# Cached sequences' attention: pages taken unsplit into float32 products, four sequences in four strips of 32 array columns

## The chip, the core and the metric

One NeuronCore of a Trainium2 chip runs one program. TensorE (PE; PEld is its weight load) multiplies, VectorE (DVE), ScalarE (ACT) and GpSimd (POOL) do the element work, and SyncE (SP) issues the transfers. The metric is the device time of one execution in microseconds (us), lower is better.

## The reference, cut to what matters

One step of a two-layer decoder for a prompt of 1024 tokens and for 8 sampled sequences of 4 new tokens. The first layer's mixer has a differential attention: four heads, two maps of 64 channels each, values of 128 channels. Each of the 8 sequences also attends to 2048 cached tokens, in 16 pages of 128 that a page table names:

```python
s = jnp.einsum('bqhcd,bkhcd->bhcqk', q.astype(jnp.float32), k.astype(jnp.float32)) * scale
s = jnp.where(visible, s, -jnp.inf)
p = jax.nn.softmax(s, axis=-1)
w = p[:, :, 0] - lam * p[:, :, 1]
return jnp.einsum('bhqk,bkhe->bqhe', w, v.astype(jnp.float32))
```

A page holds 128 tokens by 512 numbers (four heads by two maps by 64, or four heads by 128), 256 KB. All 128 pages of keys and 128 pages of values are read once, in float32. Beside the attention the mixer has a convolution branch; then come an output product, an MLP, the second layer (a state-space mixer) and its MLP.

## The kernel before, in words

Nearly all products are made of float32r parts: a number is split into a high part of 12 bits (a copy to float32r on ScalarE) and the rest (a subtraction on VectorE or GpSimd), and each product becomes two or three products of parts. Tiles of [128, 1056] ("slabs", 48 of them) hold everything; eight banks of PSUM hold [128, 512] each.

The first layer's attention has three streams, which `mixer0` starts at lines 1495 to 1513. The main line is `prompt` (the prompt's own attention, block by block: scores `sp`, maximum and exponential, weights `p`, their transposes `wT`, outputs `av`). Beside it run generators that `pump` advances by rates: `decode_k` (rate RK), `decode_v` (rate RV), the softmax `dec_softmax` between them, and later `conv_half`, the convolution's part of the output product. The generators set the order in which work is written; a scheduler with a model of the engines then sets each engine's final order.

`decode_k`, in steps of two pages of one sequence: the pages `pg` are turned (`kT`, eight transposes, L920), the high parts copied from PSUM (`pgh`, L923), the low parts subtracted (`pgl`, L929). The 32 rows of queries of one sequence (8 per head: two maps by four tokens) stand with high and low parts, and with the places of two sequences, in 128 columns of weights (`QB`); per head one product with the high keys (L963) and one with the low (L964), 256 keys wide, add up in the bank `sc`. Two sequences share 64 rows. ScalarE copies the half of the high queries (L968), VectorE adds that of the low ones (L969). After 32 of the 64 steps four sequences' scores stand in `SA` and `SB`, and `dec_softmax` makes their weights, transposes them and splits them (`PT`, L1087, L1088), 64 columns per sequence.

`decode_v`, in steps of two pages of one sequence: high copy (L995, ScalarE), low subtraction (L999, by turns on GpSimd and VectorE), then per page two products of 64 columns of weights with 512 values (L1034, L1035), all adding up in the bank `O` of that sequence. `heads_of` picks the heads' blocks out.

Of the kernel before, what the change touches and what calls it, by code (L numbers as in the profile page):

```python
# [16 lines left out]
P = 128  # L17
# [31 lines left out]
class Step:  # L49
# [34 lines left out]
    def V(self, n):  # L84
        """n columns of a slab that is kept while any of it is in use"""
        if self.vn + n > T:
            self.vs, self.vn = self.S("keep"), 0
        v = self.vs[:, self.vn:self.vn + n]
        self.vn += n
        return v  # L90

    def dma(self, out, in_):
        """a transfer of the queue that keeps the order of the program"""
        i = self.nc.sync.dma_start(out, in_)
        self.tc.keep_in_program_order(i)
        self.last_dma = i.ins
        return i

# [34 lines left out]
    def gains(self, names):  # L133
        """generator: the gains' loads, then the gains on the feature axis"""
# [18 lines left out]
    def newton(self, out, m):  # L153
        """out = m ** -0.5: the table's value, and one Newton step; m is used up"""
# [6 lines left out]
    def factor_of(self, out, ssq):  # L161
        """out = -(ssq / D + 1e-6) ** -0.5: the table's value, and one Newton step"""
# [7 lines left out]
    def colsum(self, s, n):  # L170
        """sum over the partitions of s[:, :n], on every partition (in PSUM)"""
# [7 lines left out]
    def wprep(self, src, k, m, eng=None):  # L179
        """weights [128, k, m], split exactly into two float32r parts"""  # L180
# [31 lines left out]
    def split(self, hi, lo, x, scale=None):  # L212
        """hi + lo = x * scale, both of 12 bits"""
# [8 lines left out]
    def x_load(self, c):  # L222
        """the rows of a chunk of x"""
# [9 lines left out]
    def x_factor(self, xs, c, r):  # L233
        """generator: the norm's factor of a chunk's tokens, on every partition; the rows are used up"""
# [19 lines left out]
    def x_rows(self, xs, c, x, r):  # L254
        """generator: a chunk of x on the feature axis: the residual, the split operand, with the factor r or without"""
# [37 lines left out]
    def res_load(self, res, c):  # L293
        """the residual of a chunk: three tiles to a slab"""
# [8 lines left out]
    def post(self, y, c, s, gk, l, h, nxt):  # L303
        """generator: h += rmsnorm(y); for the next layer: its split operand, its factor and the residual"""
# [28 lines left out]
    def end(self, y, c, s, gk, l, h):  # L333
        """generator, a step to each product: the last chunk of the outputs, normed on the token axis"""
# [82 lines left out]
    def factor(self, n):  # L417
        """the norm's factors of the next n chunks"""
# [5 lines left out]
    def chunk_ready(self, c):  # L424
        """before the first products of a stage with a chunk"""
# [11 lines left out]
    def store(self, y, c):  # L437
        """generator: a chunk of the outputs"""
# [16 lines left out]
    def ffn_seq(self, G):  # L455
        """the units of weights in their order: ("u", tile), ("d", first tile, tiles, part). The last sum is of four"""
# [24 lines left out]
    def ffn(self, l, X, r, res, nxt, G, early=None):  # L481
        """squared-ReLU MLP; G: tiles of hidden rows that one sum in PSUM takes"""
# [75 lines left out]
    def gemm_prep(self, w):  # L558
        """the weights of a square product, tile by tile: the first ones ahead of it"""
# [10 lines left out]
    def gemm_post(self, w, Z, gk, l, res, nxt, early=None):  # L570
        """h += rmsnorm(Z w), then what the next layer takes of it"""
# [29 lines left out]
LEADK, LEADV, VM, VP, RK, RV, SMW = 6, 4, 2, (0,), 3.5, 1.5, 6.0  # L601
# [4 lines left out]
VL = ()  # L606
TH, RC, RE = 24, 1.0, 1.0
HL, KA, VA, SL = 17, 2, 2, 1.0
# [3 lines left out]
class Step0(Step):  # L612
    """the attention and convolution mixer of the first layer"""

# [1 line left out]
    def consts0(self):  # L616
        """generator: the loads, then the rest"""
# [19 lines left out]
        # bits of the row: t = p & 3, c = (p >> 2) & 1, s = p >> 5  # L637
# [6 lines left out]
        # first and last column that a row sees: 4 s, 4 s + t  # L644
# [12 lines left out]
        # causal mask of a diagonal block, as a product with the identity  # L657
# [8 lines left out]
        # lambda, on every partition  # L666
# [6 lines left out]
        # gains of the normed heads, of the convolution's norm, both negated, and its taps  # L673
# [16 lines left out]
    def lam(self):  # L690
        """the maps' factors"""
# [3 lines left out]
        # co = -lambda; rowco = 1 or -lambda, by the row's map  # L695
# [7 lines left out]
    def conv_state(self):  # L703
        """generator: the last 30 rows of each sequence, on the channel axis, ahead of the new ones"""
# [17 lines left out]
    def conv(self, k, u, acc):  # L722
        """generator: the 31 taps of one tile of channels"""
# [3 lines left out]
        # the samples: every window against the taps, then the sum  # L727
# [15 lines left out]
    def conv_rest(self, tiles, rest):  # L743
        """generator: the other taps of each tile"""
# [13 lines left out]
    def convs(self, tiles, cd):  # L758
        """generator: the tiles of channels in turn, as they come, then their norm"""
# [20 lines left out]
    def conv_out(self, u):  # L780
        """generator: the convolution's new states"""
# [17 lines left out]
    def rows_rsqrt(self, sq, n, m, r):  # L799
        """generator: r = -(column sums of sq / m + 1e-5) ** -0.5, on every partition; sq is used up"""  # L800
# [13 lines left out]
    def conv_norm(self, acc, s, cd):  # L814
        """generator: layer norm over the channels, silu; s: the channels' sum over the tiles"""
# [25 lines left out]
    def out_units(self, half):  # L841
        """the output product's weights for half of its rows, in units of two tiles of columns"""
# [9 lines left out]
    def conv_half(self, cd, y):  # L852
        """generator: the convolution's part of the output product"""
# [23 lines left out]
    def page_numbers(self, i, n):  # L877
        """entries i to i+n of the page table, for the addresses of transfers"""
# [7 lines left out]
    def pages(self, x, high, low, item):  # L886
# [3 lines left out]
        raw, half, cut = {}, {}, {}  # L890
# [7 lines left out]
        def first(i):  # L898
            if i < 64:
                rw = raw.pop(i)  # L900
                cut[i] = self.S("pgh", F32R), self.S("pgl", F32R)
                half[i] = high(rw, *cut[i])

        def second(i):
            if i < 64:
                low(i, half.pop(i))

        return load, first, second, cut

    def decode_k(self, qs, ks):  # L910
        """generator: the new tokens over the pages of keys. qs: split queries in blocks, ks: the new keys"""
        nc = self.nc

        def high(rw, hi, lo):
            hv, lv = (z[:, :1024].rearrange("p (h j t) -> p h j t", h=4, j=2) for z in (hi, lo))
            parts = []
            for j in range(2):
                pt = self.PS("kT")
                for h in range(4):
                    nc.tensor.transpose(pt[:, h * P:(h + 1) * P], rw[:, 512 * j + h * P:512 * j + (h + 1) * P],  # L920
                                        self.ident)
                pv = pt.rearrange("p (h t) -> p h t", h=4)
                nc.scalar.copy(hv[:, :, j, :], pv)  # L923
                parts.append((lv[:, :, j, :], pv, hv[:, :, j, :]))
            return parts

        def low(i, parts):
            for p in parts:
                nc.vector.tensor_sub(*p)  # L929

        def place(i):
            """the pair of sequences, the step, the sequence of the pair"""
            return i // 16, i % 16 // 2, i % 2

        def item(i):
            sp, pr, e = place(i)
            return 8 * (2 * sp + e) + pr

        load, first, second, cut = self.pages("k", high, low, item)
# [3 lines left out]
        for i in range(KA):  # L943
            first(i)
            second(i)
        for i in range(64):
            g, n = i // 32, i % 32
            load(i + LEADK)
            first(i + KA)
            yield 0.9  # L950
            second(i + KA)
            hi, lo = cut.pop(i)
            sp, pr, e = place(i)
            rows = slice(64 * (sp % 2), 64 * (sp % 2) + 64)
            if n == 0:
                SA, SB = self.S("SA"), self.S("SB")
            q = pr % 2
            if q == 0 and e == 0:
                sc = self.PS("sc")
            for h in range(4):  # L960
                lh = qs[h][:, 2 * sp + e, :]
                o = sc[:, 256 * q:256 * q + 256]
                nc.tensor.matmul(o, lh, hi[:, 256 * h:256 * h + 256], start=e == 0 and h == 0, stop=False)  # L963
                nc.tensor.matmul(o, lh, lo[:, 256 * h:256 * h + 256], start=False, stop=e == 1 and h == 3)  # L964
            if q == 1 and e == 1:
# [1249 lines left out]
```

## Time and profile before

| | us |
|---|---|
| median of 3 runs | 2844.65 (2844.02 to 2846.12) |
| span of the profiled execution, first to last instruction | 2835.7 |
| the stretch of the cached attention in it, from 340 to 712 | 372 |

| engine | busy us | share of the span |
|---|---|---|
| PE | 2607.7 | 92% |
| PEld | 2506.6 | 88% |
| DVE | 1762.2 | 62% |
| ACT | 1101.3 | 39% |
| POOL | 998.6 | 35% |

PE's ends are modelled and its matmuls overlap, so the mean duration of a matmul is longer than the distance from one start to the next; where work of PE is counted, the distance of starts counts. PE is the busiest engine over the whole span, but the shares differ by stage: in the stretch from 500 to 712 PE stands idle for about a fifth of the time.

### The profile page before, as it was taken

The numbers are of one execution on the slowest core, as the hardware profiler recorded it, in microseconds if no ns is written. First come the engines' busy times: TensorE is split into PE (matmuls) and PEld (weight loads), VectorE is DVE, ScalarE is ACT, GpSimd is POOL, SyncE is SP. The second block draws the span as 40 slices with busy tenths as digits, with TensorE's granted clock in tenths as the row PEclk, the third lists the DMA queues.
The fourth block names the chain that finished last, engine by engine and source line by source line (L and its number), as shares of the span: only waits on it lengthen the run. The fifth ranks groups of instructions, "written<-read, shape, count | busy, mean of one in ns | idle before, by whom it ended". The sixth has DMA issues, their size and how long they took to land. (4 is left out here: it accounts for less than half of the span.)

```text
span 2835.7 us, 41961 instructions
## 1 busy us (share of the span) xinstructions
PE 2607.7 (92%) x15955; PEld 2506.6 (88%) x15955; DVE 1762.2 (62%) x2943; ACT 1101.3 (39%) x2199; POOL 998.6 (35%) x1177
## 2 busy tenths in 40 slices
PE   8965999877989999999999888799889999999998
PEld 7965988754979999999999877599889999999997
DVE  6999689887486755565554799962571333333335
ACT  6322477766544121212222466652443122112213
POOL 2887101355151687435320668821420000000004
PEclk9977999989999999999999999899999999999999
DMA  6102587764303122312231343213131111111121
GB/s 189 33 24 92 182 267 223 232 204 152 124 13 122 56 87 85 87 60 91 81 105 55 104 143 119 83 53 105 36 114 45 45 45 45 45 45 45 52 86 68
DMA packets 243680, 272.42 MB, mean 96 GB/s; under 512 B 26324, under 2 KB 179682, under 8 KB 243471
## 3 DMA queue, kind: packets, MB, share of 16 engines
q1 hardware_dynamic: 243147, 269.51, 30.0%
q8 instruction: 126, 2.06, 0.3%
q14 instruction: 75, 0.61, 0.1%
q10 hardware_dynamic: 332, 0.23, 0.0%
HBM read 215.86 MB, written 54.26 MB: 95 GB/s over the span
## 5 line engine op out<-in xcount | busy, mean ns | idle before, releaser
L193 PE MATMUL mm<-hh,whi 128*128 128x352 f32 x1536 | 500.8, 326 | 0.0
L195 PE MATMUL mm<-hh,wlo 128*128 128x352 f32 x1536 | 496.7, 323 | 0.0
L194 PE MATMUL mm<-hl,whi 128*128 128x352 f32 x1536 | 496.4, 323 | 0.0
L193 PE MATMUL mm<-zh,whi 128*128 128x352 f32 x1344 | 447.6, 334 | 0.2 <-DVE y L537 0.2
L194 PE MATMUL mm<-zl,whi 128*128 128x352 f32 x1344 | 439.3, 327 | 3.0 <-DVE zl L217 3.0
L195 PE MATMUL mm<-zh,wlo 128*128 128x352 f32 x1344 | 438.2, 326 | 0.0
L291 POOL TENSOR_TENSOR ssq<-ssq,sq 128x352 f32<-128x352 f32 x72 | 72.9, 1012 | 939.4 <-issue 672.5
L503 ACT ACTIVATE t<-t 128x352 f32<-128x352 f32 x192 | 95.4, 498 | 736.1 <-DVE t L502 735.8
L537 DVE TENSOR_TENSOR y<-y,mm 128x352 f32<-128x352 f32 x456 | 230.5, 518 | 238.4 <-PE mm L195 236.4
L187 DVE TENSOR_TENSOR wlo<-wraw,whi 128x1024 fp32r<-128x1024 f32 x160 | 205.0, 1284 | 186.3 <-ACT whi L186 185.4
L193 PE MATMUL mm<-gh,whi 128*128 128x352 f32 x960 | 313.8, 327 | 0.0
L194 PE MATMUL mm<-gl,whi 128*128 128x352 f32 x960 | 311.7, 325 | 0.0
L195 PE MATMUL mm<-gh,wlo 128*128 128x352 f32 x960 | 311.6, 325 | 0.0
L186 ACT CAST whi<-wraw 128x1024 fp32r<-128x1024 f32 x180 | 187.1, 1043 | 290.5 <-DMA wraw<-in_w_ffn_up 103.7
L194 PEld LDWEIGHTS mm<-hl,whi 128*128 128x128 f32 x1536 | 289.9, 189 | 0.5 <-issue 0.2
L193 PEld LDWEIGHTS mm<-hh,whi 128*128 128x128 f32 x1536 | 289.6, 189 | 0.6 <-issue 0.2
L195 PEld LDWEIGHTS mm<-hh,wlo 128*128 128x128 f32 x1536 | 289.6, 189 | 0.0
L194 PEld LDWEIGHTS mm<-zl,whi 128*128 128x128 f32 x1344 | 257.4, 191 | 6.8 <-DVE zl L217 4.3
L193 PEld LDWEIGHTS mm<-zh,whi 128*128 128x128 f32 x1344 | 257.1, 191 | 3.3 <-issue 0.9
L195 PEld LDWEIGHTS mm<-zh,wlo 128*128 128x128 f32 x1344 | 256.4, 191 | 0.2
L502 DVE SCALAR_TENSOR_TENSOR t<-mm,r 128x352 f32<-128x352 f32 x192 | 99.9, 523 | 222.0 <-PE mm L195 220.5
L193 PE MATMUL mm<-xh,whi 128*128 128x352 f32 x480 | 164.0, 344 | 31.5 <-DVE proj L1377 23.4
(513 smaller groups left out, 5474.7 us busy)
## 6 DMA issues: line engine op xcount, KB each, us to landing
pg<-in_cache_k SPq DMA_DIRECT2D x128, 256.0 KB
pg<-in_cache_v SPq DMA_DIRECT2D x128, 256.0 KB
wraw<-in_w_ffn_up SPq DMA_DIRECT2D x64, 512.0 KB
wraw<-in_w_ffn_down SPq DMA_DIRECT2D x64, 512.0 KB
hres<-res SPq DMA_DIRECT2D x24, 528.0 KB
res<-y SPq DMA_DIRECT2D x24, 528.0 KB
wraw<-in_w_in_even SPq DMA_DIRECT2D x20, 512.0 KB
tabs<-tc SPq DMA_DIRECT2D x16, 512.0 KB
```

Of the source, the lines that this page charges most:

```text
L186: nc.scalar.copy(hi[:, :n], raw[:, :n])
L187: (eng or nc.vector).tensor_sub(lo[:, :n], raw[:, :n], hi[:, :n])
L193: nc.tensor.matmul(out, wh, xh, start=first, stop=False)
L194: nc.tensor.matmul(out, wh, xl, start=False, stop=False)
L195: nc.tensor.matmul(out, wl, xh, start=False, stop=last)
L291: (nc.vector if k in YV else nc.gpsimd).tensor_add(s, s, q)
L502: nc.vector.scalar_tensor_tensor(t1, pt, 0.0, r[:, chunk(c)], op0=ALU.max, op1=ALU.mult)
L503: nc.scalar.activation(t1, t1, AF.Square)
L537: nc.vector.tensor_add(yc, yc, pt)
```

## The change

The pages are no longer split. Keys are turned and copied once (first half of a step on ScalarE, second on VectorE); values go from the page into the product. The products are plain float32. Steps go through four sequences in turn: when all four have their two pages, sixteen products of keys (four heads by four sequences), or eight of values, are written, each with 32 columns of weights and with its result in 32 partitions of the same bank, the sequence's strip. Queries and weights stand once, unsplit. The scores of four sequences leave PSUM in one copy. The value pages are loaded eight steps ahead (four before), and the rate RV is 3.0 (1.5 before).

```diff
-LEADK, LEADV, VM, VP, RK, RV, SMW = 6, 4, 2, (0,), 3.5, 1.5, 6.0
+LEADK, LEADV, RK, RV, SMW = 6, 8, 3.5, 3.0, 6.0
...
         def load(i):
             if i < 64:
+                g, pr, s = i // 32, i % 32 // 4, i % 4
                 raw[i] = self.S("pg")
-                for j, v in enumerate(self.page_numbers(2 * item(i), 2)):
+                for j, v in enumerate(self.page_numbers(16 * (4 * g + s) + 2 * pr, 2)):
...
     def decode_k(self, qs, ks):
...
+        def turn(i, j):
+            if i >= 64:
+                return
+            if j == 0:
+                turned[i] = self.S("kt")
+            tv = turned[i][:, :1024].rearrange("p (h j t) -> p h j t", h=4, j=2)
+            pt = self.PS("kT")
+            for h in range(4):
+                nc.tensor.transpose(pt[:, h * P:(h + 1) * P], raw[i][:, 512 * j + h * P:512 * j + (h + 1) * P], self.ident)
+            pv = pt.rearrange("p (h t) -> p h t", h=4)
+            if j == 0:
+                nc.scalar.copy(tv[:, :, j, :], pv)
+            else:
+                nc.vector.tensor_copy(tv[:, :, j, :], pv)
+                del raw[i]
+        def strips(sc, g, cols, rhs):
+            for h in range(4):
+                for s in range(4):
+                    nc.tensor.matmul(sc[32 * s:32 * s + 32, cols], qs[:, h, 4 * g + s, :], rhs(s, h), start=h == 0, stop=h == 3)
...
             load(i + LEADK)
+            for j in range(2):
+                turn(i + KA, j)
+                yield 0.6
...
+            if s < 3:
+                continue
             q = pr % 2
+            if q == 0:
                 sc = self.PS("sc")
+            kts = [turned.pop(i - 3 + e) for e in range(4)]
+            strips(sc, g, slice(256 * q, 256 * q + 256), lambda s, h: kts[s][:, 256 * h:256 * h + 256])
+            kts = None
+            if q == 1:
                 p2 = pr // 2
+                nc.scalar.copy((SA if p2 < 2 else SB)[:, 512 * (p2 % 2):512 * (p2 % 2) + 512], sc)
+            yield 2.4
...
     def decode_v(self, vs, aS):
...
+                for e in range(4):
+                    nc.tensor.matmul(O[32 * e:32 * e + 32, :], tn[:, 32 * e:32 * e + 32], vs, start=True, stop=False)
+            if s < 3:
+                continue
+            pgs = [raw.pop(i - 3 + e) for e in range(4)]
             for j in range(2):
                 kt = 2 * pr + j
+                w = PT[kt // 8][:, kt % 8, :]
+                for e in range(4):
+                    nc.tensor.matmul(O[32 * e:32 * e + 32, :], w[:, 32 * e:32 * e + 32], pgs[e][:, 512 * j:512 * j + 512],
+                                     start=False, stop=kt == 15)
+                yield 2.0
...
     def dec_softmax(self, g, SA, SB):
...
+            tv = PT[-1][:, 4 * (q % 2):4 * (q % 2) + 4, :]
+            nc.scalar.copy(tv, pt.rearrange("p (k r) -> p k r", k=4))
```

On TensorE, a group of key products before: `sc` is the bank of scores, `pgh` and `pgl` are the two parts of a turned page, `QB` the queries, one number per head; the last column is the form of the result's rows by columns.

```order
L920 MATMUL kT_3075<-ident,pg_2816 128x128 x4
L920 MATMUL kT_3081<-ident,pg_2816 128x128 x4
L963 MATMUL sc_3093<-pgh_2957,QB_905 128x256
L964 MATMUL sc_3093<-pgl_2958,QB_905 128x256
L963 MATMUL sc_3093<-pgh_2957,QB_906 128x256
L964 MATMUL sc_3093<-pgl_2958,QB_906 128x256
L963 MATMUL sc_3093<-pgh_2957,QB_907 128x256
L964 MATMUL sc_3093<-pgl_2958,QB_907 128x256
```

The same place on TensorE in the changed kernel: `kt` is a turned page pair, one number per sequence, and the result has 32 rows.

```order
L926 MATMUL sc_2938<-kt_2747,QB_905 32x256
L926 MATMUL sc_2938<-kt_2760,QB_905 32x256
L926 MATMUL sc_2938<-kt_2781,QB_905 32x256
L926 MATMUL sc_2938<-kt_2824,QB_905 32x256
...
L915 MATMUL kT_3007<-ident,pg_2773 128x128 x4
L926 MATMUL sc_2938<-kt_2864,QB_905 32x256
L915 MATMUL kT_3026<-ident,pg_2816 128x128 x4
L926 MATMUL sc_2938<-kt_2912,QB_905 32x256
L1254 MATMUL tok_3033<-ident,proj_2269 128x128
```

The first four rows (sixteen in all, four for each head) belong to a whole group: neighbours differ in the sequence, and so in the strip. The rows behind them belong to the next group: single products of one strip stand between transposes of full width. Over the whole kernel the 424 products of strips stand in 61 unbroken runs, 23 of which hold one product.

On TensorE, value products before, in the second half: `O` is the bank of one sequence's outputs, `PT` the weights.

```order
L1035 MATMUL O_5724<-pgl_5866,PT_5013 64x512
L1034 MATMUL O_5724<-pgh_5921,PT_5046 64x512
L1029 MATMUL O_6076<-vS_913,PTn_5094 64x512
L1030 MATMUL O_6076<-vS_913,PTn_5094 64x512
L1147 MATMUL sp_6085<-kh__919_5875,qp_5874 128x256
```

And in the changed kernel: the values come straight from the loaded pages `pg`, four sequences in turn.

```order
L989 MATMUL O_5800<-pg_5521,PT_5719 32x512
L989 MATMUL O_5800<-pg_5529,PT_5719 32x512
L989 MATMUL O_5800<-pg_5537,PT_5719 32x512
L989 MATMUL O_5800<-pg_5545,PT_5719 32x512
...
L989 MATMUL O_5800<-pg_5870,PT_5719 32x512
L1158 MATMUL wT_5935<-ident,p_5794 128x128 x4
```

There is no operand `pgl` or `pgh` any more, and one bank `O` takes four sequences.

On VectorE, beside the keys before: each page has its subtraction (L929), and the sums of the scores' halves stand between them.

```order
L929 TENSOR_TENSOR pgl_3405<-kT_3412,pgh_3404 128x4x128
L1155 TENSOR_REDUCE pst_3378<-sp_3421 128x1
L1158 TENSOR_SCALAR pst_3378<-pst_3378 128x1
L969 TENSOR_TENSOR SB_2861<-sc_3300,SB_2861 64x512
L1158 TENSOR_SCALAR pst_3378<-pst_3378 128x1
L1188 TENSOR_TENSOR pst_3378<-pst_3378 128x1
L929 TENSOR_TENSOR pgl_3455<-kT_3456,pgh_3454 128x4x128
```

In the changed kernel VectorE copies every second page (L920) and has no row for the scores' halves.

```order
L920 COPY kt_3072<-kT_3079 128x4x128
L1104 TENSOR_REDUCE pst_3141<-sp_3142 128x1
L1104 TENSOR_REDUCE pst_3141<-sp_3145 128x1
L920 COPY kt_3111<-kT_3118 128x4x128
L1107 TENSOR_SCALAR pst_3141<-pst_3141 128x1
```

VectorE has 64 such copies in place of 128 subtractions, and the prompt's small rows stand closer together.

## Rows read from the trace of the kernel before

**Rows 1.** Busy time by stretch, with granted clock, DMA share and GB/s.

```profile
340.00:500.00 160.00, 151.39 (x1203) 140.34 (x1202) 136.03 (x299) 115.92 (x262) 12.74 (x23) 1.00 0.75 242
500.00:580.00 80.00, 67.29 (x458) 53.36 (x456) 75.35 (x126) 61.84 (x123) 30.57 (x16) 1.00 0.79 242
580.00:712.00 132.00, 98.61 (x483) 67.98 (x484) 102.51 (x184) 86.21 (x183) 70.80 (x57) 0.88 0.54 169
340.00:712.00 372.00, 317.29 (x2141) 261.69 (x2140) 313.89 (x608) 263.96 (x567) 114.11 (x95) 0.96 0.68 216
```

**Rows 2.** Groups of TensorE, 340 to 712: busy, mean ns, idle before them and releasers.

```profile
L963 PE MATMUL sc<-pgh,QB 128*128 128x256 f32 x256 | 68.1, 295 | 2.1 <-DVE SA L969 1.4 <-DVE pgl L929 0.6
L964 PE MATMUL sc<-pgl,QB 128*128 128x256 f32 x256 | 66.6, 294 | 0.0
L1035 PE MATMUL O<-pgl,PT 128*64 128x512 f32 x128 | 55.9, 438 | 26.1 <-POOL pgl L999 12.2 <-DVE pgl L999 10.3 <-DVE keep L1192 2.3
L1034 PE MATMUL O<-pgh,PT 128*64 128x512 f32 x128 | 54.0, 423 | 1.9 <-ACT pgh L995 1.9
L1224 PE MATMUL av<-v,wT 128*128 128x128 f32 x236 | 31.2, 289 | 0.5 <-DVE pgl L929 0.5
L1209 PE MATMUL wT<-ident,p 128*128 128x128 f32 x129 | 22.4, 291 | 10.9 <-DVE p L1195 8.6 <-DVE pst L1161 1.9 <-DVE keep L1237 0.4
L978 PE MATMUL sc<-sm,QB 128*128 128x256 f32 x32 | 4.7, 289 | 1.1 <-DVE SB L969 1.1
```

**Rows 3.** TensorE in order of time: start, length, instruction; keys, then values.

```profile
501.67 0.28 PE L963 MATMUL sc<-pgh,QB 128*128 128x256 f32 x1
501.79 0.28 PE L964 MATMUL sc<-pgl,QB 128*128 128x256 f32 x1
...
502.27 0.28 PE L964 MATMUL sc<-pgl,QB 128*128 128x256 f32 x1
...
701.22 0.39 PE L1148 MATMUL sp<-kl__1106_6826,qp 128*128 128x512 f32 x1
701.45 0.40 PE L1035 MATMUL O<-pgl,PT 128*64 128x512 f32 x1
...
702.60 0.40 PE L1034 MATMUL O<-pgh,PT 128*64 128x512 f32 x1
```

**Rows 4.** VectorE's groups, 340 to 712.

```profile
L929 DVE TENSOR_TENSOR pgl<-kT,pgh 128x512 fp32r<-128x512 f32 x128 | 83.3, 682 | 7.9 <-ACT pgh L923 6.6 <-PE O L1035 0.9
L999 DVE TENSOR_TENSOR pgl<-pg,pgh 128x1024 fp32r<-128x1024 f32 x32 | 51.2, 1602 | 6.0 <-ACT pgh L995 5.9
L969 DVE TENSOR_TENSOR SA<-sc,SA 64x512 f32<-64x512 f32 x8 | 5.6, 694 | 0.3
L969 DVE TENSOR_TENSOR SB<-sc,SB 64x512 f32<-64x512 f32 x8 | 5.6, 694 | 0.3
L1088 DVE TENSOR_TENSOR PT<-pT,PT 128x512 fp32r<-128x512 f32 x8 | 5.3, 678 | 0.0
```

**Rows 5.** ScalarE's two groups of page copies, 340 to 712.

```profile
L923 ACT CAST pgh<-kT 128x512 fp32r<-128x512 f32 x128 | 70.0, 602 | 26.3 <-PE kT L920 24.0 <-DMA pg<-in_cache_k 1.7
L995 ACT CAST pgh<-pg 128x1024 fp32r<-128x1024 f32 x64 | 66.1, 1055 | 8.7 <-issue 4.3 <-PE O L1034 1.3 <-DVE pgl L999 1.3
```

**Rows 6.** The copies of the tile wT: min/median/max ns, first and last start.

```profile
L1215 DVE COPY wT<-wT x24: 268/616/693, 366.3 to 723.9; 128x512 f32<-128x512 f32 x12, 128x256 f32<-128x256 f32 x4, 128x128 f32<-128x128 f32 x4, 128x384 f32<-128x384 f32 x4
```

**Rows 7.** Plain float32 products of 264 columns in time, and their durations by line.

```profile
1675.14 1.06 PE L2035 MATMUL y<-w,mt 128*128 128x264 f32 x4
...
L2035 PE MATMUL y<-w,mt x128: 383/386/647, 1675.1 to 1864.8; 128*128 128x264 f32 x128
```

**Rows 8.** Four small transposes of 31 columns in time, and their durations by line.

```profile
48.94 0.41 PE L677 MATMUL cp<-ident,cw 31*128 31x31 f32 x4
...
L677 PE MATMUL cp<-ident,cw x4: 219/220/221, 48.9 to 49.1; 31*128 31x31 f32 x4
```

More of the change, by code (lines that the diff above doesn't have):

```diff
@@ L896, in load @@
                     self.dma(raw[i][:, 512 * j:512 * j + 512], src[bass.ds(v, 1)].rearrange("o p d -> p (o d)"))
[L898 to L908, printed above, removed]
+        return load, raw
     def decode_k(self, qs, ks):
         nc = self.nc
[L914 to L939, printed above, removed]
+        load, raw = self.pages("k")
+        turned = {}
+        def turn(i, j):
[13 more added lines that the diff above has]
+                del raw[i]
@@ L943, in decode_k @@
         for i in range(KA):
-            first(i)
-            second(i)
+            for j in range(2):
+                turn(i, j)
         for i in range(64):
-            g, n = i // 32, i % 32
+            g, pr, s = i // 32, i % 32 // 4, i % 4
             load(i + LEADK)
[L949 to L955, printed above, removed]
+            for j in range(2):
+                turn(i + KA, j)
+                yield 0.6
+            if pr == 0 and s == 0:
                 SA, SB = self.S("SA"), self.S("SB")
+            if s < 3:
+                continue
             q = pr % 2
-            if q == 0 and e == 0:
+            if q == 0:
                 sc = self.PS("sc")
[L960 to L965, printed above, removed]
-                p2 = pr // 2
-                d = (SA if p2 < 2 else SB)[rows, 512 * (p2 % 2):512 * (p2 % 2) + 512]
-                nc.scalar.copy(d, sc[0:64, :])
-                nc.vector.tensor_add(d, sc[64:128, :], d)
-            yield 0.9
-            if pr == 7 and e == 1:
+            kts = [turned.pop(i - 3 + e) for e in range(4)]
+            strips(sc, g, slice(256 * q, 256 * q + 256), lambda s, h: kts[s][:, 256 * h:256 * h + 256])
+            kts = None
+            if q == 1:
+                p2 = pr // 2
+                nc.scalar.copy((SA if p2 < 2 else SB)[:, 512 * (p2 % 2):512 * (p2 % 2) + 512], sc)
+            yield 2.4
+            if pr == 7:
                 while not self.kready:
@@ L991, in decode_v @@
         nc = self.nc
-        done, late = 0, []
-        def high(rw, hi, lo):
-            nc.scalar.copy(hi[:, :1024], rw[:, :1024])
-            return lo[:, :1024], rw[:, :1024], hi[:, :1024]
-        def low(i, p):
-            (nc.gpsimd if i % VM in self.vp else nc.vector).tensor_sub(*p)
-        load, first, second, cut = self.pages("v", high, low, lambda i: i)
+        load, raw = self.pages("v")
         while not self.ready:
@@ L1005, in decode_v @@
             load(i)
+        late = None
         for i in range(64):
-            g, n = i // 32, i % 32
+            g, pr, s = i // 32, i % 32 // 4, i % 4
             load(i + LEADV)
-            fresh = []
-            while done <= i + VA:
-                first(done)
-                fresh.append(done)
-                done += 1
-            yield 0.4
-            for e in fresh:
-                second(e)
-            hi, lo = cut.pop(i)
-            s, pr = n // 8, n % 8
-            s1 = s % 2
@@ L1048, in heads_of @@
+                yield 2.0
+            pgs = None
+            if late is not None and pr == 1:
+                self.heads_of(late, g - 1, aS)
+                late = None
+                yield 0.5
+            if pr == 7:
+                late = self.S("ob")
+                nc.scalar.copy(late[:, :512], O)
+        yield 1.0
+        self.heads_of(late, 1, aS)
+    def heads_of(self, ob, g, aS):
         nc = self.nc
@@ L1431, in put_v @@
                 self.dma(o["new_v_sample"][0].rearrange("b t h d -> (b t) (h d)"), st[:n, :512])
[L1432 removed]
+                nc.scalar.copy(vS[:NS, :], st[:NS, :512])
         first = []
```

100 lines of the change are left out of this document (27 added, 73 removed).

## Prediction

> **What bounds the kernel now.** I read the busy time by stretch first, then TensorE's groups with what ended their idle time, then the starts of single products in order of time, and then the other engines' groups. The cached attention lies between 340 and 712 of the profiled span, 372 us [rows 1]. From 340 to 500, where the keys are, TensorE is busy 151.4 of 160 us: it is the bound, and only fewer or shorter products help. From 500 to 580 VectorE is busy 75.4 of 80 and TensorE only 67.3: the bound is VectorE. From 580 to 712 neither is full (TensorE 98.6, VectorE 102.5 of 132) and the granted clock falls to 0.88, so that TensorE's work runs there for about a quarter of the time at the lower of its two levels (1.2 in place of 2.4 GHz). TensorE's idle time over the three stretches is 8.6 + 12.7 + 33.4 = 54.7 us. Of that 26.1 + 1.9 = 28.0 us stand before the value products, and what ended them are the subtractions `pgl` on GpSimd and VectorE and the copies `pgh` [rows 2].
>
> The work of TensorE is counted by the distance of starts. Key products: 0.60 us for five steps, 0.12 each; value products: 1.15 us for five steps, 0.23 each [rows 3]. So before, 544 products of keys take 65 us and 272 of values 63, together 128 us [rows 2, 3]. The rest of the stage's work is 372 - 54.7 idle - 16 lost to the clock (0.12 of 132) - 128 = 173 us, which the change leaves alone.
>
> **The change, part by part.**
>
> *Splits removed.* VectorE loses the 128 key subtractions (83.3), its 32 value subtractions (51.2), the sums of halves (11.2) and the split of the weights (5.3): 151 us [rows 4]. It gains 64 copies of 128x512 from PSUM, and the wide copies `wT`, the nearest row, take up to 0.69 us: 44 us [rows 6]. Net 107 of its 314 us in the stage. ScalarE loses 66 us of value copies and half of the 70 us for keys [rows 5]. GpSimd loses all value subtractions. None of these engines can then bound the stage: VectorE would have some 207 us in it, ScalarE about 160.
>
> *Waits removed.* The 28.0 us before the value products have no cause left: a value product then waits for its page and for the weights only. Behind it the next to be late are the prompt's own weights (8.6 us of waits for `p` [rows 2]) and the four pages of a group, so I give back 22 of the 28. With TensorE fuller the clock falls less; I take half of the 16 us, 8. The other 27 us of idle time in the stage are chains of the prompt; an emptier VectorE shortens them, and I take 7 us.
>
> *Wait added.* A group of sixteen key products waits for the copy of the fourth sequence's page. Behind it on TensorE stand the next transposes and the prompt's scores. Before, the same place already waits for `pgl`, two engines in a row; now it is one copy. The transposes run two steps ahead. Bounds: 0 to 11 us (16 groups by one copy of 0.69 [rows 6]); I take 3, nearer to nothing, because of the two steps.
>
> *The products themselves.* This is the term that decides. A plain float32 product shows two records in the trace, each with a weight load: 64 products at the line of `y` give 128 records. Their starts lie (1.06 - 0.386)/3 = 0.225 us apart for 264 columns [rows 7], 0.85 ns per column and record, so 0.218 for 256 and 0.436 for 512. In the changed kernel 256 key products of 256 columns, 32 of 32 columns and 136 value products of 512 columns make 848 records. The floor of a small record is (0.41 - 0.220)/3 = 0.063 us [rows 8].
> - One after the other: 512 x 0.218 + 64 x 0.063 + 272 x 0.436 = 234 us, 106 more than before.
> - All four strips at once: 512 x 0.063 (the floor is above 0.218/4) + 64 x 0.063 + 272 x 0.109 = 66 us; in the 23 runs of one product nothing overlaps, which costs 11 more: 77 us, 51 less than before.
> - Two at a time: the second record of a product needs the same strip as its first and must follow it, and in every row here products start in the order of the program. So while the second record of one strip streams, the first record of the next strip can start, and no more: each product costs one record's time, and each of the 61 runs one record more at its end: 137 us, 9 more than before.
>
> No product in this trace goes beside another in the array, so the rows only bound this term: from -51 to +106. I take the middle case, +9, since it is the one that follows from two records per product and starts in order.
>
> The Trainium skill, "TensorE: Matmul & The Clock Gate", Part 3 (Packing small matmuls), says that products in different column strips run at the same time, with 2.38x measured for three strips, and that matmuls start and end strictly in order. By its speedup alone the 234 us would be about 98, an estimate from that figure; its rule of order leads to the middle case. No run here shows either yet.
>
> *The sum.* +9 - 22 - 8 - 7 + 3 = -25 us against the profiled span of 2835.7: 2811. The median of the runs is 9 us above this span, as the time around the first and last instruction is in it, so 2844.65 - 25 = **2820 us**. The stage has no cover behind it: after 712 TensorE goes on with the convolution's half of the output product without a gap, so what the stage saves or loses reaches the end in full.
>
> **The rivals.**
>
> *No overlap.* The strips' products run one after the other. Then +106 - 22 - 8 - 7 - 15 + 0 = +54, where the 15 is idle time that the longer products fill: 2899 us, slower. It decides as soon as two neighbours overlap by less than about 1.4: 234/1.4 = 167 is 39 more than before, what the other terms give back. For it: every product in the trace of before is spaced by its own length, even two into the same bank. Against it: neighbours in a run go into different partitions of the bank and different columns of the array [the order of the changed kernel shows it], so nothing but the order of issue binds them.
>
> *All four at once.* -51 for the products; the stage would hold 173 + 77 = 250 us of TensorE work. Then the transfers come near to binding: they are busy 0.68 of 372 = 253 us now [rows 1], and the same pages must come. With some 15% over that, the stage takes about 300: -72, 2773 us. For it: the four strips need nothing of each other. Against it: two records on the same strip in a row hold up whatever stands behind them if starts are in order.
>
> *The array empties at each change of kind.* A float32 product of 264 columns lasts 0.386 and streams for 0.220 or so; the other 0.166 is its way through the array [rows 7]. In the trace of before it is hidden by the next product. If a change between full width and strips cannot hide it, 122 changes (both ends of 61 runs) cost 20 us: 2840, no change that could be told. For it: 23 runs of a single product, so many changes. Against it: from a product of 128 columns of weights to one of 64 the starts lie 0.23 us apart, as within either kind (701.22 to 701.45 [rows 3]).
> The Trainium skill, "TensorEngine Tiling (Array Packing)", Key Properties, says that a change of the tiling mode drains TensorE. That speaks against the change, and by it this case is the rule; no row of before changes the mode, as far as it shows.
>
> **How the numbers follow.** Forecast 0.40; no overlap 0.27; all four 0.21; emptying 0.12. A difference of under 0.2% (5.7 us) cannot be told from none in this kernel. The forecast's own range is 2795 to 2838. The no-overlap case spreads from 2875 to 2925, the four-strip case from 2750 to 2800. The range of 2762 to 2902 takes in the forecast, the emptying case, most of the four-strip case and half of the slow one, about 0.83. Faster: nearly all of the forecast and all of the four-strip case, a quarter of the emptying one: 0.61. Same: 0.10, from the emptying case and the forecast's upper end. Slower: 0.29, the no-overlap case and a little of the emptying one.
>
> **What would show it.** The distance of starts in a run of key products: 0.218 per product of two records is two at a time, 0.436 is none, about 0.13 all four. A first gap of about 0.17 us at each end of a run is the emptying. Idle time of TensorE before value products should fall from 28 us to under 8, VectorE's busy time in the stage from 314 to about 207, the granted clock from 580 to the end of the stage should be near 0.95, and the value products should end before the convolution's half begins. The prediction is wrong if the strips' starts lie a whole product apart, if value products wait for pages as long as they waited for subtractions, or if the scheduler's order leaves TensorE waiting for the copies of keys.

## The result and the profile after

| | before | after |
|---|---|---|
| median of 4 runs each, us | 2844.66 | 2778.14 (2776.59 to 2779.17) |
| span of the profiled execution, us | 2835.7 | 2776.0 |

The ratio is 0.9766, with an interval of 0.9752 to 0.978: 66.5 us less, where 25 were forecast. 6.8 of the 66.5 come of the choice of the profiled execution (median less span: 9.0 before, 2.1 after; in repeats of the kernel before, an execution of 2845.18 has a span of 2842.9, so most of the 9 is not, as the prediction has it, time around the first and last instruction). The traces have 59.7 us to explain.

The stage gave all of it. The next products behind it, the transposes `aT`, start at 739.1 us before and at 676.9 after, 62.2 earlier; 2.5 us are lost again by the end. The busy times by stretch of the changed kernel, to be read against [rows 1] (columns: stretch, length, then busy us and instructions of PE, PEld, DVE, ACT and POOL, then PE's granted clock, share of DMA time, GB/s):

```profile
340.00:500.00 160.00, 151.99 (x1364) 114.59 (x1362) 101.62 (x237) 93.95 (x223) 7.61 (x21) 0.99 0.90 293
500.00:580.00 80.00, 71.33 (x512) 42.30 (x509) 42.34 (x116) 35.73 (x101) 7.96 (x21) 0.94 0.97 311
580.00:660.00 80.00, 65.18 (x378) 47.78 (x378) 50.61 (x131) 42.95 (x120) 9.47 (x21) 0.89 0.38 127
580.00:712.00 132.00, 117.18 (x724) 99.70 (x724) 71.21 (x164) 69.54 (x172) 20.55 (x45) 0.94 0.40 128
340.00:712.00 372.00, 340.50 (x2596) 256.60 (x2595) 215.17 (x517) 199.22 (x496) 36.12 (x87) 0.96 0.73 238
```

VectorE is no longer full in the second stretch (42.3 of 80, against 75.4). While pages load, the transfers are busy 0.90 and then 0.97 of the time. And from 580 to 660, where the value products end (the last starts at 601.8), TensorE is idle for 14.8 of 80 us and its clock falls to 0.89: there the prompt's chains stand with nothing of the cached attention beside them.

TensorE's groups of the changed kernel from 340 to 712, and VectorE's and ScalarE's for the pages (busy, mean ns, idle before and what ended it):

```profile
L915 PE MATMUL kT<-ident,pg 128*128 128x128 f32 x512 | 70.5, 278 | 6.9 <-DMA pg<-in_cache_k 4.8 <-ACT p L1120 1.3 <-ACT t L1177 0.6
L989 PE MATMUL O<-pg,PT 128*32 128x512 f32 x256 | 46.7, 598 | 0.6 <-DMA pg<-in_cache_v 0.6
L926 PE MATMUL sc<-kt,QB 128*32 128x256 f32 x512 | 42.8, 384 | 0.2 <-DVE kt L920 0.2
L1158 PE MATMUL wT<-ident,p 128*128 128x128 f32 x144 | 25.4, 301 | 16.5 <-DVE p L1144 9.5 <-DVE pst L1140 3.8 <-DVE pst L1137 2.4
L920 DVE COPY kt<-kT 128x512 f32<-128x512 f32 x64 | 43.5, 686 | 30.2 <-PE kT L915 26.4 <-DMA pg<-in_cache_v 3.2 <-DMA pg<-in_cache_k 0.2
L918 ACT COPY kt<-kT 128x512 f32<-128x512 f32 x64 | 37.5, 592 | 54.7 <-PE kT L915 42.1 <-issue 8.7 <-DMA pg<-in_cache_k 3.2
```

The 28 us before value products [rows 2] are 0.6, the wait for `kt` is 0.2. Against [rows 2], where the key products' two lines were busy 134.7 and the values' 109.9, the strips are busy 42.8 and 46.7, though each product is now two records (512 and 256). How that can be is seen in the order of time (start, length, instruction): one run of sixteen key products, and below it single value products between transposes.

```profile
363.78 1.93 PE L926 MATMUL sc<-kt,QB 128*32 128x256 f32 x32
365.65 0.44 PE L1158 MATMUL wT<-ident,p 128*128 128x128 f32 x2
...
524.12 1.02 PE L989 MATMUL O<-pg,PT 128*32 128x512 f32 x2
525.07 0.66 PE L915 MATMUL kT<-ident,pg 128*128 128x128 f32 x4
525.65 1.04 PE L989 MATMUL O<-pg,PT 128*32 128x512 f32 x2
526.63 0.44 PE L915 MATMUL kT<-ident,pg 128*128 128x128 f32 x2
```

32 records stand in 1.93 us, of which the last lasts 0.38: (1.93 - 0.38)/31 = 0.050 us from start to start. That is a quarter of the 0.218 a record of 256 columns takes: four strips at once. The single starts in this run show it too: the first four records, one for each strip, start within 0.02 us, the next four 0.24 after the first four, and so on every 0.216. So the second record of the first product starts behind the first records of the three products that follow it in the program. A product that stands alone takes 525.07 - 524.12 = 0.95 us for two records of 512 columns.

Summing, line by line, the distance from each start to the next (idle time apart) from 340 to the start of `aT`: products of keys and values 148 before, 86 after, -62 (some of it at the lower clock before); all other work of TensorE 196 and 219, +23; idle time 55 and 31, -23. Together -62, by which the stage is shorter.

### The profile page after: what moved, and what is told of

Its sections match the earlier page's. It is cut to its first block, busy times and chain, and to the rows that moved or that the text cites. A ratio compares the mean times of both kernels' runs of the same rounds, so it can differ in the third digit from the quotient of the medians.

```text
span 2776.0 us, 41481 instructions
## 1 busy us (share of the span) xinstructions
PE 2564.8 (92%) x15979; PEld 2435.9 (88%) x15979; DVE 1629.7 (59%) x2784; ACT 996.5 (36%) x2029; POOL 904.0 (33%) x1141
## 5 line engine op out<-in xcount | busy, mean ns | idle before, releaser
L738 DVE SCALAR_TENSOR_TENSOR acc<-proj,keep,acc 128x1024 f32<-128x1024 f32 x84 | 190.9, 2274 | 2.0
```

The costliest lines, as they stand in the source:

```text
L738: nc.vector.scalar_tensor_tensor(acc[:, :NP], u[:, i:i + NP], w[:, k, i:i + 1], acc[:, :NP], op0=ALU.mult, op1=ALU.add)
```

## The experiments

Theory A: four strips run at once, each change between strips and full width has a price, and the rest of the gain is the removed waits. Rival B: products overlap two at a time only. Rival C: the gain is mostly the freed VectorE and ScalarE. All ratios are to the kernel before.

**The products by themselves.** A kernel with runs of 32 products of 256 columns at its end:

```diff
+        for i in range(32):  # in turn; then [0:32]; then i % 2; then i // 4 % 4
+            nc.tensor.matmul(pt[32 * (i % 4):32 * (i % 4) + 32, :256], w[:, 32 * (i % 4):32 * (i % 4) + 32], r, start=True, stop=True)
+        for i in range(16):  # strip and full width in turn; then both full width
+            nc.tensor.matmul(pt[0:32, :256], w[:, 0:32], r, start=True, stop=True)
+            nc.tensor.transpose(pt[:, 0:P], x[:, 0:P], self.ident)
```

> The changed kernel, with bare products added behind its last output on TensorE (their results go nowhere): 32 float32 products of 256 columns with 32 columns of weights, four strips in turn; all in one strip; two strips in turn; four in a row per strip; single strip products between full-width transposes; full-width products between transposes; 64-column strips in turn; float32r with 64 columns. Theory A (each strip takes its own stream, four at once): 0.05 to 0.055 us per record in turn, 0.218 in one strip, 0.109 with two strips and with 64 columns. Theory B (starts in order, a second record of a strip holds up all behind it): 0.109 with four strips or two, 0.218 in one. Four in a row per strip: A with a queue for each strip 0.055, A with issue in order 0.19, B 0.19. Strip product and transpose in turn: 0.44 + 0.11 = 0.55 us a pair if a change of kind is free, 0.75 or more if the array empties at each change; the full-width pair 0.55 in either case.

TensorE in order of time in that kernel: four strips in turn (L2042), one strip (L2045), two in turn (L2048), each strip four products in a row (L2051), then a strip product and a transpose in turn (L2054, L2055) and the same at full width (L2058, L2059).

```profile
2803.05 3.66 PE L2042 MATMUL bench<-bx,bw 128*32 128x256 f32 x64
...
2811.98 14.00 PE L2045 MATMUL bench<-bx,bw 128*32 128x256 f32 x64
...
2831.26 7.10 PE L2048 MATMUL bench<-bx,bw 128*32 128x256 f32 x64
...
2843.64 8.17 PE L2051 MATMUL bench<-bx,bw 128*32 128x256 f32 x64
...
2857.09 0.62 PE L2054 MATMUL bench<-bx,bw 128*32 128x256 f32 x2
2857.64 0.33 PE L2055 MATMUL bench<-ident,bx 128*128 128x128 f32 x1
2857.89 0.62 PE L2054 MATMUL bench<-bx,bw 128*32 128x256 f32 x2
...
2875.09 0.59 PE L2058 MATMUL bench<-bx,bw 128*128 128x256 f32 x2
2875.52 0.27 PE L2059 MATMUL bench<-ident,bx 128*128 128x128 f32 x1
2875.63 0.60 PE L2058 MATMUL bench<-bx,bw 128*128 128x256 f32 x2
```

With the last record's 0.38 taken off and 63 distances: 0.052 us per record in four strips, 0.107 in two, 0.216 in one. Rival B, which gives 0.109 in four strips, is out. Two strips of 64 columns in turn (L2062) also give 0.107. Four products in a row on one strip give 0.124: starts in the order of the program would give (7 x 0.216 + 0.052)/8 = 0.195, strips that hold up nobody 0.054. The single starts tell why: each strip goes on every 0.216 us, and the first record of the next strip starts 0.006 us behind the fifth of the eight records of the strip before (blocks begin 0.89 us apart, at 2843.64, 2844.53, 2845.43). So three of the eight wait at their strip without holding up the next, and they start later than a record behind them in the program; whether three is a limit of the strip or of the engine stays open. A strip product with a transpose takes 0.81 us, a full-width one 0.54 (means of the fifteen distances from pair to pair): two changes of kind cost 0.27 us here, 0.15 of it from the transpose to the strip and 0.12 back. Between products of 512 columns and a run of strips, by the starts at the runs' ends, the two come to 0.21: the price depends on the neighbour.

The Trainium skill, "TensorE: Matmul & The Clock Gate", Part 3 (Packing small matmuls), gives 2.38x for three strips; here four give 0.216/0.052 = 4.1x and two give 2.0x. Its rule that matmuls start and end strictly in order does not hold for the starts here, as the single records show, and taken for the time it led to rival B.

**One strip after the other.** The changed kernel with the products of a group ordered by strip (for values likewise):

```diff
-            for h in range(4):
-                for s in range(4):
+            for s in range(4):
+                for h in range(4):
```

> The same products in another order: all four heads (keys) or both pages (values) of one sequence before the next sequence, so that neighbours share a strip. Theory A with issue in order (overlap needs neighbours in different strips): a group of sixteen key products takes about 6.3 in place of 1.9 us, a group of eight value products 5.7 in place of 3.5: +70 and +35 us of TensorE, of which the stage hides little: 2850 to 2885. Theory A with a queue for each strip: as the changed kernel, 2778. Theory C (the gain comes from the splits and waits that went, the products hardly matter): 2780 to 2800.

2809.5 (0.9879, 0.9862 to 0.9895), 31 us slower than the changed kernel. A run of key products in its trace, against 1.93 us:

```profile
368.07 4.59 PE L926 MATMUL sc<-kt,QB 128*32 128x256 f32 x32
```

(4.59 - 0.38)/31 = 0.136 per record. The first records of the four strips start 0.89 us apart, as in the bench, and 3 x 0.89 + 7 x 0.216 = 4.19 of the 4.21 us. The order alone is worth 31 us of the 66. The time fell between the expectations for the reason the bench gave: by distance of starts the products take 137 us and not 86, where issue in order would have added 105.

**Keys alone, values alone.** One half of the new code and one of the old (decode_k new, decode_v old, and the reverse), with what each needs of queries and weights.

> Only the keys changed (strips, one copy a page); values as before, split, LEADV 4, RV 1.5. Theory A (the gain lies in the products, 62 us of TensorE time for both): keys give some 25 us less product time and free VectorE for the value splits: 2810 to 2820. Theory C (the gain lies in the waits for the value splits, 28 us): keys alone keep those waits: 2835 to 2845.

> Only the values changed (strips, no split, LEADV 8, RV 3.0); keys as before, split. Theory A: half of the product time and all of the waits before the values: 2800 to 2812. Theory C: nearly the whole gain, 2780 to 2790.

Keys 2818.7 (0.9909, 0.9892 to 0.9926), -25.5; values 2803.3 (0.9861, 0.9845 to 0.9877), -40.8. Both lie in Theory A's ranges and outside C's. Their sum is -66.3, the whole change: neither half needs the other. The values' half includes the raised rate, whose price is found below. With the keys alone TensorE still waits some 25 us for the value splits.

**More changes of kind.** The eight transposes that stand ahead of a group of key products are put inside it: 87 unbroken runs of strips, 61 before.

```diff
             for h in range(4):
+                if between is not None:
+                    between(h)          # two transposes of the page to come
                 for s in range(4):
```

> The changed kernel, with the eight transposes of a key page that stand ahead of a group of 16 strip products spread through the group, two ahead of every four products. The same instructions, 87 unbroken runs of strip products in place of 61. Theory A with a price for each change of kind (0.27 us for a pair of changes, as measured by itself): 26 x 0.27 = 7 us more, 2785. Rival (a change of kind costs nothing in the kernel, since the next weights load beside it): 2778, within 2 us.

2780.8 (0.9784, 0.9771 to 0.9798), with medians 2.6 us apart and intervals that overlap the changed kernel's: unclear by time. The trace of this kernel tells more:

```profile
366.57 0.44 PE L919 MATMUL kT<-ident,pg 128*128 128x128 f32 x2
366.94 0.63 PE L934 MATMUL sc<-kt,QB 128*32 128x256 f32 x4
367.49 0.44 PE L919 MATMUL kT<-ident,pg 128*128 128x128 f32 x2
367.86 0.64 PE L934 MATMUL sc<-kt,QB 128*32 128x256 f32 x8
```

By distance of starts the transposes and key products together take 110.5 us in place of 102.4: 8.1 for 26 runs, 0.31 each, near the 0.27 of the bench. But TensorE's idle time fell from 31.3 to 26.7, so over half of it came out of time that was idle anyway. The price is real. Of the 23 us of other work above it explains only a part: the change back to full width stands in the strips' own 86 us, and the change into strips, 0.09 to 0.15 by the bench, makes 6 to 9 us in 61 runs. Most of the rest goes with the old rate, below.

**Fewer runs, more pages ahead.** Keys loaded 10 and transposed 6 ahead (`LEADK` 10, `KA` 6), the value products of two pages without a break: 51 runs.

> The changed kernel, with key pages loaded 10 ahead and not 6, transposed 6 ahead and not 2, and the eight value products of two pages issued without a break: 51 unbroken runs of strip products in place of 61. If a change of kind costs 0.27 us a pair: 10 x 0.27 = 2.7 us less, and the waits for copies of kt and for pages (0.2 and 4.8 us in the trace) go too: 2772 to 2776. If the transfers, busy 0.9 of the time while pages load, already set the stage: 2778, no change.

2768.3 (0.9734, 0.9721 to 0.9747), 9.9 less than the changed kernel, more than either theory gave. This edit changes several things, and they were not parted.

**The splits' work put back.** The products stay as changed, VectorE and ScalarE again do subtractions and copies of the old size, which nobody reads; the edit for keys:

```diff
+            z = self.S("idle", F32R)[:, :512].rearrange("p (h t) -> p h t", h=4)
+            if j == 0:
+                nc.vector.tensor_sub(z, pv, tv[:, :, j, :])
+            else:
+                nc.scalar.copy(z, pv)
```

> The changed kernel, with the elementwise work of the old splits put back on VectorE and ScalarE, its results read by nobody (for keys 64 subtractions of 512 columns on VectorE and 64 copies on ScalarE, for values 32 copies and 32 subtractions of 1024 columns). Theory A (TensorE sets the stage, and the products' time is what went): VectorE is busy 158 of 270 us while pages load, with room for some 80 us more, so 0 to 8 us come back: 2778 to 2786. Rival C (the freed VectorE and ScalarE are what made the gain: their results come sooner): 20 us or more come back: over 2798.

2803.0 (0.9853, 0.9838 to 0.9869): 25 us back. Theory A's "0 to 8" was wrong. Either these engines count in the whole stage, or (theory D) only at its end, where nothing stands beside the chains; the same work at the old rate, below, parts the two.

**The old rate.** The changed kernel with `RV` 1.5 and 4 value pages ahead, and with the rate alone:

```diff
-LEADK, LEADV, RK, RV, SMW = 6, 8, 3.5, 3.0, 6.0
+LEADK, LEADV, RK, RV, SMW = 6, 4, 3.5, 1.5, 6.0     # rate only: 6, 8, 3.5, 1.5, 6.0
```

> The changed kernel, with value pages loaded 4 ahead and not 8, and the value part's rate 1.5 and not 3, as before the change. Theory A (the gain is the products' own time, four strips at once): only the waits of the value products come back, at most the 23 us of idle time that the trace of the changed kernel lost, more likely 2 to 10 us: 2780 to 2788. Rival C (the gain came from pages ahead and from the order, and the products only fill what was idle): 20 us or more come back: over 2798.

> The changed kernel with the value part's rate 1.5 as before the change, but pages 8 ahead as in the changed kernel. Theory D (with rate 3 the value products are done early, and the end of the stage has too little left beside its chains: TensorE was idle 31 us from 340 us to the end of the stage, 9 us with the old rate and the old 4 pages ahead): the rate alone gives the 24 us, 2751 to 2758. Rival (4 pages ahead in place of 8 made it, by fewer transfers in flight at once): no gain here, 2774 to 2782.

2753.8 (0.9681, 0.9666 to 0.9696) and 2754.2 (0.9685, 0.967 to 0.97): both 24 us *faster* than the changed kernel, and the best here. Both sides of the first expectation missed the sign. The rate alone does it; 4 or 8 pages ahead makes no difference. The rate says how much value work is issued for a given amount of the prompt's. Raised to 3 it spends the value products early. The stretches of the kernel with the old rate and 4 pages:

```profile
340.00:500.00 160.00, 156.30 (x1408) 118.15 (x1410) 105.58 (x246) 97.31 (x233) 7.28 (x21) 1.00 0.89 291
500.00:580.00 80.00, 78.49 (x544) 42.27 (x540) 53.55 (x142) 43.84 (x123) 7.96 (x21) 1.00 0.96 313
580.00:660.00 80.00, 76.00 (x486) 58.11 (x481) 45.10 (x113) 43.06 (x115) 18.39 (x42) 1.00 0.48 162
340.00:712.00 372.00, 362.80 (x2751) 270.31 (x2750) 229.84 (x538) 206.36 (x511) 47.98 (x98) 1.00 0.73 238
```

From 580 to 660 TensorE is busy 76.0 and not 65.2 us, at the full clock, as strips still stand between the prompt's steps (the last starts at 619.8). Up to `aT`, which starts at 652.1, it is idle for 8.8 us where it was 31.3. With the rate alone, and 8 pages ahead, the idle time is 17.5 us in the profiled execution, and the other work of TensorE takes 206 us in place of 219: about half of the gain is idle time there, and the rest fits the clock, 0.99 and not 0.95 from 340 to `aT`.

**The rate in the kernel before,** `RV` 3.0 and nothing else.

> The kernel before the change, with the value part's rate 3 and not 1.5 (its 4 pages ahead stay). If the higher rate leaves the end of the stage with nothing beside its chains whatever the products cost: 10 to 25 us slower, 2855 to 2870. If before's value products are held by their splits and pages and not by the rate: 2845, within 4 us.

2864.9 (1.0069, 1.0054 to 1.0085): 20 us slower. So the rate costs about the same with the old products; it is no matter of the strips. The stretch behind the last value product, up to `aT`, tells how: before, the changed kernel, the changed kernel with the old rate and 4 pages, and before with the new rate.

```profile
710.00:739.00 29.00, 28.33 (x195) 27.00 (x193) 12.34 (x31) 13.73 (x37) 6.78 (x19) 1.00 0.43 129
602.00:677.00 75.00, 61.23 (x375) 56.36 (x373) 47.99 (x120) 43.13 (x114) 16.54 (x41) 0.89 0.21 65
620.00:652.00 32.00, 31.48 (x218) 29.82 (x213) 14.83 (x38) 16.52 (x46) 6.73 (x19) 1.00 0.33 101
697.00:763.00 66.00, 54.84 (x370) 50.69 (x370) 40.50 (x111) 38.13 (x107) 17.74 (x40) 0.97 0.22 67
```

The higher rate makes this stretch more than twice as long with either kind of product, and TensorE is idle in it for 13.8 and 11.2 us, where it was 0.5 and 0.7.

**The splits' work at the old rate.** The two edits together: `RV` 1.5, 4 pages ahead, and the idle work.

> The kernel with the old rate and the old 4 value pages ahead (2753.8), with the elementwise work of the old splits put back on VectorE and ScalarE, read by nobody. Theory D (the 25 us that this work cost in the changed kernel came out of the end of the stage, where TensorE waits for VectorE with nothing beside): with the background work spread out there is something to run meanwhile, and it costs under 10 us: 2754 to 2764. Rival C (VectorE and ScalarE set the stage's pace whatever the order): 20 us or more again, over 2774.

2792.5 (0.9821, 0.9806 to 0.9836): 38.7 us slower than without that work. Theory D's "under 10" fell too: this work costs whatever the order. The idle time that it adds lies beside the value products, 8.7 to 37.8 us up to the last of them (17.7 to 34.6 at the new rate), and not behind them, 0.5 to 0.6 (13.8 to 13.1). TensorE's largest waits (total us, times, longest) and the stage's row with that work:

```profile
PE wT L1168 <- DVE p L1154: 18.3, 8, 3.5
PE wT L1168 <- DVE pst L1147: 4.4, 2, 2.4
PE sc L931 <- DVE kt L920: 2.6, 2, 1.4
PE kT L915 <- DVE idle L924: 2.4, 1, 2.4
```

```profile
340.00:712.00 372.00, 333.66 (x2518) 240.38 (x2517) 284.51 (x601) 255.74 (x577) 40.09 (x84) 0.97 0.72 231
```

and the largest wait without it:

```profile
PE wT L1158 <- DVE p L1144: 3.9, 4, 1.7
```

VectorE is busy only 284.5 of 372 us, yet TensorE waits 18.3 us for the prompt's weights `p` and not 3.9. In four of these eight waits, 10.9 us, an idle subtraction of 0.7 or 1.2 us is among the last four instructions before `p` in VectorE's queue, and the engine goes without a gap of over 0.04 us into `p`. The idle work does not load the engines only: it also keeps banks of `kT` and slabs of pages longer. The waits that it ends itself come to 6.5 us; what the slabs cost was not parted from the rest. Up to `aT` its idle time is 38.2 and not 8.8, +29.4 of the 40.5 by which `aT` is later (692.6); the clock, 0.97 for 1.00, is in the rest.

**Old rate and fewer runs.** The two edits that helped (`RV` 1.5, 8 value pages ahead, with the edits of the fewer runs): 55 runs.

> The changed kernel with the value part's rate 1.5, key pages loaded 10 ahead, transposed 6 ahead, and the eight value products of two pages issued without a break: 55 unbroken runs of strip products in place of 61. If TensorE alone sets the stage (busy 98 per cent of it with the old rate), what is left to gain is the price of the changes of kind, 0.27 us for each run fewer: 2 to 5 us under the kernel with the old rate, 2748 to 2753. If the transfers set it: 2754 or more.

2757.9 (0.9695, 0.9682 to 0.9708): no better than the old rate alone. By the expectation the transfers would then set the stage; the trace shows waits for key pages of 5.3 us (6.6 with the old rate and 8 value pages ahead, 0.6 with 4) beside longer waits of `wT` for VectorE, so that is not shown.

## Why the prediction was wrong, step by step

The runs split the change at the old rate into 2844.4 to 2792.5 (products, the waits for the splits' results, which nobody reads there, and the part of the old work that was not put back), to 2753.8 (freed engines, with what the idle work holds), to 2778.1 (rate): -52, -39, +24.

- **The products themselves, "Two at a time", +9.** This step failed. It held that the second record of a product holds up what stands behind it, because all starts of the trace before are in order. That trace has no two neighbours in different strips, so its rows could not show it; the bench does, 0.052 and not 0.109 per record. By distance of starts the products went from 148 to 86 us, -62, some at the lower clock before: the term was 71 us off and had the wrong sign, and "faster" came out right by the other terms. Rival "All four at once" had the mechanism: its 77 us for the strips stand against 86 measured. That its 2773 is so near 2778.1 is in part luck, as it had no term for the rate either. The "floor" of 0.063 that it took for a small record was too high; 0.050 was seen.
- **"The rest of the stage's work, 173 us, which the change leaves alone".** This failed too, the other way, and is the main reason why the sum was 41 us off and not 71: the other work of TensorE rose by 23 us. Changes into strips are 6 to 9 of them; with the old rate it is 206 to 208 us, 10 to 12 above before.
- **The array empties.** Named as another case, it was true beside the four strips: 0.27 us for both ends of a run, against the 2 x 0.166 = 0.33 priced there. The forecast held 0.22 per run for another reason. The Trainium skill, "TensorEngine Tiling (Array Packing)", Key Properties, has the drain at a change of mode; the bench fits that, at 0.27 us for a pair of changes; no row shows the draining itself.
- **Waits removed, clock, prompt's chains, -22 - 8 - 7 = -37.** The idle time fell by 23 us, near the 26 that the waits, the chains and the wait added make together, but the parts are others: the waits before value products fell by 27 (to 0.6; "under 8" was named), and the idle time before `wT` rose by 6, where the chains were to give 7. The clock gave nothing in the changed kernel: 0.96 of the stretch from 340 to 712 before [rows 1] and after. With the old rate it is 1.00. The idle work's 38.7 us are no measure of these terms, as it does not bring back the waits before value products; the largest wait that it brings back is the prompt's for `p`, 14.4 us more, of which the forecast had a part in 7 for the chains.
- **The rate and the pages ahead.** The prediction gave `RV` and `LEADV` no term. The rate costs 24 us here. With it the clock from 580 is 0.94 (0.89 up to 660), where "near 0.95" was named for another reason, and the idle time before `wT` is 16.5 us after 10.9 [rows 2]; with the old rate and 4 pages they are 1.00 and 5.6.
- **Wait added, +3.** 0.2 us were seen; the copies are two steps ahead, as the step said.
- **VectorE's busy time, 207.** 215.2 from 340 to 712, in which more of the next stage now lies. The copies `kt` took 43.5 us, 44 were priced from `wT` [rows 6].
- **Transfers near to binding.** Right: 0.97 from 500 to 580. 7 us were seen waiting for `kT`, 4.8 of them for key pages. They did not bind the stage: with the old rate `aT` comes 25 us earlier with the transfers busy 0.89 and 0.96 of the two stretches.
- **No overlap,** the slower rival, did not happen; what it would have taken is the bench's 0.216 per record in one strip.

## What to carry to other kernels

A product that uses 32 of the array's columns costs a quarter if its neighbours in the program use the other three strips in turn, and over half if each strip's products stand together: interleave them, and keep them in long runs, since both ends of a run together cost 0.27 us beside transposes. When background work gets cheaper, look again at the rate at which it is spent: here the rate raised along with it cost 24 of 91 us, as TensorE ran out of it well before the chains that it covered were done. An engine at three quarters of its time can still be late for whoever waits on its queue: what counts is what stands ahead of the awaited instruction.

## What the runs showed of the hardware

- Records of plain float32 products in four strips overlap fully, though each product is two records on one strip: 0.052 us per record of 256 columns, against 0.216 in one strip.
- Three records can wait for their strip while a record of another strip behind them in the program starts; a fourth holds it up: 0.124 us with four products in a row per strip.
- Changes between strips and full width cost 0.27 us a pair beside transposes of 128 columns (0.15 in, 0.12 out) and 0.21 beside products of 512 columns.
